# A hybrid decoder step on one core: softmax scaling shared by two query blocks, later loads of left down weights, and keys of both maps split in one operation

## The chip, the cores and the metric

The kernel runs on one core of one Trainium2 chip. The metric is the device time of one execution in microseconds (us): the median of three runs of the kernel before is 1473.42 us (1473.18 to 1474.27).

## The reference, cut to what matters

One layer of a decoder trunk is computed in fp32 for a prompt of 1024 rows and eight sample rows, with a model width of 1024. It consists of a mixer with four heads of differential attention and four heads of retention, a cross-attention into 256 memory rows, a squared-ReLU MLP of width 4096, and a last norm. Two parts of it concern the change. The first is the differential attention of the prompt, causal and with a relative bias, with two softmax maps per head of 64 columns of keys each:

```python
def probs(qi, ki):
    s = jnp.einsum('bqhd,bkhd->bhqk', qi, ki).astype(f32) * scale + bias
    return jax.nn.softmax(jnp.where(mask, s, neg), axis=-1)

attn = probs(q1, k1) - lam * probs(q2, k2)
return jnp.einsum('bhqk,bkhd->bqhd', attn, v.astype(f32))
...
a = head_rms(oa) * subln.astype(jnp.float32) * (1.0 - lam_init)
```

The second is the MLP, of which the product with `w_down` is the last stage:

```python
def sq_relu_mlp(h, w_up, w_down):
    return jnp.square(jax.nn.relu(h @ w_up)) @ w_down
```

## The kernel before

**Products.** Every fp32 product is made of three TensorE products of parts: each operand is split into a high part (a rounding copy, on ScalarE) and a low part (a subtraction of the high part from the whole, on VectorE), and high times high, high times low and low times high are added in PSUM (`mm3`, L75). Most of the rows that ScalarE (ACT) and VectorE (DVE) run are such splits.

**Attention.** The four heads run one after another between about 245 and 455 us. A list of 40 items (head, pair of query blocks, group of key blocks) is walked by the loop over `g` near L1380; `x` is the item's number within its head. At each item the loop issues scores of some query block and map (`scores`, L999, where `SCORES` says which), the transposes of the next item (`turn`, L1037; tile `trA`, with its high and low parts `ah` and `al`), and the weighing of values (`weigh`, L1058; tile `av`). Products of the next head's projection (`qkp`) fill the gaps on TensorE (PE). A scheduler then orders the instructions of each engine; what stands in an engine's queue runs in that order.

`scores(h, q, m)` computes the block of 128 queries `q` against the `128(q+1)` keys that the mask leaves, for map `m`: PE writes `sp` from the key stacks `KA[m]` and `KB[m]` and the query stack `Q[m]`, DVE adds the bias and takes the row's extreme (L1019), and ACT takes the exponential with its row sum (L1025). The map's tile is `e_h_q_m`. For `m` = 1, DVE then takes a reciprocal of the second map's sum (L1032), forms the scaling with `nlam` and the first map's sum (L1033), and adds the scaled second map onto the first, in place (L1034). That last row's length is `128(q+1)` columns. The tile of the second map has the tag `e1` with two buffers.

The stacks serve both parts of a key in one product: `KA[m]` holds the high part of map `m`'s 64 rows twice (rows 0 to 63 and 64 to 127), `KB[m]` the low part twice, and `Q[m]` the high part of the queries in one half and the low part in the other. `load_part` (L961) makes them, first for 688 columns and later for 336: for each map an ACT copy of 64 rows (L967), a transfer of it to the other half issued on GpSimd's queue (L968), a DVE subtraction (L969), a transfer (L970). GpSimd (POOL) also runs the memsets of `ah` and `al`, a power function for norms (L141) and the low parts of values (L995).

The norm over a head's output uses `norm_sums` (L1075): ACT squares the outputs of the head before (`sq_0` during head 1, and so on) into a tile that has the same tag `e1`, so that it takes the buffer of the second map of block 6 of the running head; then eight products with a column of ones write `ct` (L1084).

**Down product.** It runs from about 1134 us in four passes (`g` = 0 to 3), by a Strassen-like scheme with seven products `q` of half matrices. Left operands are weights, loaded as `raw_d` (L2492) and split into `wd` (L2388, L2389). Right operands are hidden values, loaded as `raw_h` in two pieces per product from `HT` or `HQ` in device memory (L2375) and split into `UH` and `UL` (L2381, L2382). PE writes `dn` into one of eight PSUM banks in turn (L2412), and DVE adds the bank onto the sums `c` (L2546), which frees it. All these loads are issued by SyncE's queue (SP), which runs in order. `load_left` issues a pass's eight `raw_d` loads.

## Time and profile before

| What | Value |
|---|---|
| Median of three runs | 1473.42 us |
| Profiled execution, its time / its span | 1475.19 us / 1473.4 us |
| PE busy | 1455.7 us, 99% of the span |
| DVE busy | 1107.9 us, 75% |
| ACT busy | 679.7 us, 46% |
| POOL busy | 314.4 us, 21% |
| Mean granted clock of PE | 0.996 |

The profile is one execution. Its time is 1.8 us more than its span, and 1.8 us more than the median of the runs. A row of a timeline has the start and the length in us, the engine, the line of the program, the operation, what it writes and reads (buffer numbers left out), and, in brackets, how long the engine was idle before it and what released it. PE rows of matmuls overlap in their ends. The stages follow from the lines: projections until about 245 us, attention to 455 us, the rest of the mixer and the memory part, the up product, and the down product from 1134 us.

### The profile page before, as it was taken

What the parts mean: (1) busy time and instruction counts of PE and PEld (TensorE: products, weight loads), DVE (VectorE), ACT (ScalarE), POOL (GpSimd) and SP (SyncE); (2) the same over time, 40 slices, a digit from 0 to 9 for tenths busy, and PEclk for the clock granted to TensorE, in tenths of its full rate; (3) what the DMA queues carried; (4) which work ended last, traced back from release to release, by engine and by line L of the source; (5) the groups of instructions that cost most, each with busy time, mean ns of one, the idle gap of its engine ahead of it and who ended that gap; (6) DMA issues with size and microseconds to landing.
All of it is one profiled execution on the core that took longest, in us unless ns stands there. A gap on an engine that the chain in (4) does not pass through costs nothing.

```text
span 1473.4 us, 28129 instructions
## 1 busy us (share of the span) xinstructions
PE 1455.7 (99%) x11013; PEld 1401.0 (95%) x11013; DVE 1107.9 (75%) x2263; ACT 679.7 (46%) x1327; POOL 314.4 (21%) x345
## 2 busy tenths in 40 slices
PE   9999999999999999999999999999999999999998
PEld 7899779999889999999999999999999999999998
DVE  7666536888867756567868988888888878787876
ACT  7434435666552441267436533343435443343454
POOL 0035433122304511224122000000002211110380
PEclk9999999999999999999999999999999999999998
DMA  8155738215957265654762444333446764536273
GB/s 295 62 188 171 205 70 192 72 34 159 283 169 269 100 209 170 177 178 122 236 234 77 151 159 158 138 136 133 149 159 216 262 213 144 173 105 200 71 130 116
DMA packets 129833, 238.98 MB, mean 162 GB/s; under 512 B 13606, under 2 KB 80987, under 8 KB 129572
## 3 DMA queue, kind: packets, MB, share of 16 engines
q1 hardware_dynamic: 91354, 170.66, 36.0%
q0 software_dynamic: 27472, 46.93, 11.8%
q10 hardware_dynamic: 10874, 19.60, 3.5%
q8 instruction: 86, 1.41, 0.4%
q14 instruction: 47, 0.39, 0.1%
HBM read 171.13 MB, written 58.92 MB: 156 GB/s over the span
## 4 chain that ended last, share of the span: by engine, by line
PE 88%; DVE 5%; DMA 2%; ACT 2%; issue 1%; POOL 0%; ACTq 0%; SPq 0%; DVEq 0%
PE dn L2412 20%; PE Z L2244 9%; PE qkp L75 6%; PE Y L2244 6%; PE X L2244 6%; PE mq L75 6%; PE pr_m L75 6%; PE pr_o L75 5%; PE grp L75 3%; PE sp L75 2%; PE mv L75 2%; PE mk L75 1%; PE av L75 1%; PE mpv L75 1%; PE vap_z L524 1%; PE vrp_z L524 1%
## 5 line engine op out<-in xcount | busy, mean ns | idle before, releaser
L2412 PE MATMUL dn<-UH,wd 128*128 128x258 f32 (+1 forms) x1800 | 326.6, 283 | 3.0 <-DVE c L2546 3.0
L2412 PEld LDWEIGHTS dn<-UH,wd 128*128 128x128 f32 x1800 | 279.6, 190 | 3.6 <-ACT wd L2388 2.6
L2412 PE MATMUL dn<-UL,wd 128*128 128x258 f32 x900 | 254.6, 283 | 0.0
L2412 PEld LDWEIGHTS dn<-UL,wd 128*128 128x128 f32 x900 | 170.5, 189 | 0.1
L2546 DVE TENSOR_TENSOR c<-c,dn 128x258 f32<-128x258 f32 (+1 forms) x217 | 89.1, 417 | 38.5 <-PE dn L2412 35.8
L2270 ACT ACTIVATE hq<-r 128x258 f32<-128x258 f32 x128 | 53.7, 421 | 117.4 <-DVE r L2269 117.3
L2244 PE MATMUL Z<-T_h,wu 128*128 128x258 f32 x512 | 98.1, 283 | 0.0
L2244 PE MATMUL X<-UH,wu 128*128 128x258 f32 x512 | 97.5, 282 | 0.0
L2388 ACT CAST wd<-raw_d 128x512 fp32r<-128x512 f32 x96 | 58.7, 619 | 82.0 <-PE dn L2412 77.3
L2052 ACT CAST wu<-raw_up 128x512 fp32r<-128x512 f32 x96 | 59.0, 616 | 61.0 <-PE Z L2244 52.6
L2381 ACT CAST UH<-raw_h 128x1032 fp32r<-128x1032 f32 x56 | 58.7, 1055 | 55.2 <-PE dn L2412 27.9
L2244 PEld LDWEIGHTS X<-UH,wu 128*128 128x128 f32 x512 | 81.3, 188 | 0.0
L2244 PEld LDWEIGHTS Z<-T_h,wu 128*128 128x128 f32 x512 | 81.3, 189 | 0.0
L2382 DVE TENSOR_TENSOR UL<-raw_h,UH 128x1032 fp32r<-128x1032 f32 x56 | 72.9, 1301 | 9.9 <-ACT UH L2381 9.9
L2389 DVE TENSOR_TENSOR wd<-raw_d,wd 128x512 fp32r<-128x512 f32 x96 | 72.3, 759 | 10.2 <-ACT wd L2388 10.2
L2281 POOL DMA_DIRECT2D HT<-ht x32 | 17.2, 536 | 292.1 <-DVE ht L2280 291.6
L2244 PE MATMUL Z<-T_l,wu 128*128 128x258 f32 x256 | 72.3, 282 | 0.0
L2244 PE MATMUL X<-UL,wu 128*128 128x258 f32 x256 | 72.3, 282 | 0.0
L129 ACT CAST wh_u<-raw_u 128x1024 fp32r<-128x1024 f32 x43 | 44.7, 1047 | 57.6 <-PE mq L75 39.9
L2053 DVE TENSOR_TENSOR wu<-raw_up,wu 128x512 fp32r<-128x512 f32 x96 | 64.8, 689 | 3.6 <-ACT wu L2052 3.6
L2402 POOL TENSOR_TENSOR raw_d<-raw_d,raw_d 128x512 f32<-128x512 f32 x16 | 22.1, 1384 | 197.0 <-DVE raw_d L2398 145.3
L130 DVE TENSOR_TENSOR wl_u<-raw_u,wh_u 128x1024 fp32r<-128x1024 f32 x39 | 48.6, 1257 | 20.2 <-ACT wh_u L129 20.0
(616 smaller groups left out, 4707.4 us busy)
## 6 DMA issues: line engine op xcount, KB each, us to landing
raw_u<-in_wall SPq DMA_DIRECT2D x49, 512.0 KB
HT<-ht POOLq DMA_DIRECT2D x32, 516.0 KB, 3.0
raw_h<-HT SPq DMA_DIRECT2D x32, 516.0 KB
raw_up<-in_wall SPq DMA_DIRECT2D x32, 512.0 KB
raw_d<-in_wall SPq DMA_DIRECT2D x32, 512.0 KB
HQ<-hq ACTq DMA_DIRECT2D x32, 387.0 KB
raw_h<-HQ SPq DMA_DIRECT2D x24, 516.0 KB
cmk<-in_cmk SPq DMA_DIRECT2D x16, 512.0 KB
```

What stands on the lines that cost most here:

```text
L75: pinned(nc.tensor.matmul(out, l, r, start=start, stop=stop))
L130: (lo_engine or nc.vector).tensor_sub(wl[:, :n], raw[:, :n], wh[:, :n].bitcast(F32))
L2052: nc.scalar.copy(w[:, :512], src)
L2053: nc.vector.tensor_sub(w[:, 512:], src, w[:, :512].bitcast(F32))
L2244: pinned(nc.tensor.matmul(ps, l, r[:, k, :], start=first and k == 0 and x == 0, stop=k == 3 and x == 2, skip_group_check=True))
L2270: nc.scalar.activation(h[:, PLACE[quad], :], r, AF.Square)
L2381: nc.scalar.copy(h, rv)
L2382: nc.vector.tensor_sub(l, rv, h.bitcast(F32))
L2388: nc.scalar.copy(w[:, :512], src)
L2389: nc.vector.tensor_sub(w[:, 512:], src, w[:, :512].bitcast(F32))
L2412: pinned(nc.tensor.matmul(ps[:, part], l, r[:, k, cq], start=first and k == 0 and x == 0, stop=k == 3 and x == 2, skip_group_check=True))
L2546: nc.vector.tensor_add(y, y, ps)
```

## The change

There are three edits.

**Keys.** For heads 1 to 3, one ACT copy of 128 rows writes both maps' high parts into `KA[1]`, and one DVE subtraction of 128 rows writes both low parts into `KB[1]`. Two transfers on GpSimd's queue bring map 0's half from there into both halves of `KA[0]`, two more into both halves of `KB[0]`, and with each query split one more transfer copies map 1's half within `KA[1]` or `KB[1]`. Head 0 is loaded as before. For each part there are six transfers where there were four, one ACT copy where there were two, and one DVE subtraction where there were two.

**Scaling.** The scaling and the addition onto the first map are left out for even query blocks and made with those of the odd block that follows: one reciprocal and one scaling of two columns serve both, then two additions run, the even block's first.

**Down weights.** In the pass `g` = 1, the eight `raw_d` loads are put behind the last load that was issued so far on SP's queue.

```diff
--- before.py
+++ after.py
@@ -961,7 +961,17 @@
         def load_part(h, cs):
             KA, KB, Q, _ = stacks[h]
             qraw, kraw = raws[h]
-            for m in range(2):
+            lo, hi = slice(0, 64), slice(64, 128)
+            if h:
+                nc.scalar.copy(KA[1][:, cs], kraw[:, cs])
+                for x in (lo, hi):
+                    nc.gpsimd.dma_start(KA[0][x, cs], KA[1][lo, cs])
+                nc.vector.tensor_sub(KB[1][:, cs], kraw[:, cs], KA[1][:, cs].bitcast(F32))
+                yield
+                for x in (lo, hi):
+                    nc.gpsimd.dma_start(KB[0][x, cs], KB[1][lo, cs])
+                yield
+            for m in range(0 if h else 2):
                 own = slice(64 * m, 64 * m + 64)
                 oth = slice(64 - 64 * m, 128 - 64 * m)
                 nc.scalar.copy(KA[m][own, cs], kraw[own, cs])
@@ -974,6 +984,9 @@
                 oth = slice(64 - 64 * m, 128 - 64 * m)
                 nc.scalar.copy(Q[m][own, cs], qraw[own, cs])
                 nc.vector.tensor_sub(Q[m][oth, cs], qraw[own, cs], Q[m][own, cs].bitcast(F32))
+                if h:
+                    K1 = (KA, KB)[m][1]
+                    nc.gpsimd.dma_start(K1[lo, cs], K1[hi, cs])
                 yield
 
         vraws = {}
@@ -1027,11 +1040,15 @@
             )
             seen["ACT"] = nc.cur_bb.bb.instructions[-1]
             if m:
-
-                e0 = es[h, q][0]
-                nc.vector.reciprocal(mn[:, 2:3], sm[:, 1, q : q + 1])
-                nc.vector.scalar_tensor_tensor(mn[:, 3:4], mn[:, 2:3], nlam, sm[:, 0, q : q + 1], ALU.mult, ALU.mult)
-                nc.vector.scalar_tensor_tensor(e0[:, :n], e[:, :n], mn[:, 3:4], e0[:, :n], ALU.mult, ALU.add)
+                es[h, q] += (e,)
+            if m and q % 2:
+                nc.vector.reciprocal(mn[:, 2:4], sm[:, 1, q - 1 : q + 1])
+                nc.vector.scalar_tensor_tensor(mn[:, 2:4], mn[:, 2:4], nlam, sm[:, 0, q - 1 : q + 1], ALU.mult, ALU.mult)
+                for x in range(2):
+                    e0, _, e1 = es[h, q - 1 + x]
+                    w = P * (q + x)
+                    nc.vector.scalar_tensor_tensor(
+                        e0[:, :w], e1[:, :w], mn[:, 2 + x : 3 + x], e0[:, :w], ALU.mult, ALU.add)
                 seen["E"] = nc.cur_bb.bb.instructions[-1]
 
         def turn(h, pr, kg):
@@ -2492,7 +2509,8 @@
                         nc.sync.dma_start(raws[p][x][:, :1024], i["wall"][U_DN + 8 * g + 2 * p + x])
                 seen["SP"] = nc.cur_bb.bb.instructions[-1]
 
-            load_left((0, 1) if g == 0 else range(4))
+            with tc.issue_after(seen["SP"]) if g == 1 else nullcontext():
+                load_left((0, 1) if g == 0 else range(4))
             S, W, bank, copied = {}, {}, {}, {}
 
             parts = [((1, 2), (1, 2), (0, 1)), ((), (1, 2), (2, 3)), ((6,), (6,), (0, 1)), ((), (6,), (2, 3))]
```

On ACT in head 2, around the square of head 1's outputs (`sq_1`; `e_2_7_1` is the exponential of block 7's second map, `raw_o0` a unit of weights for a later product), the order before is:

```order
L1025 ACTIVATE e_2_7_0_3999,sm_2_3471<-e_2_7_0_3999,mn_2_7_4000 128x1024
L1077 ACTIVATE sq_1_4038<-oraw_1_3286 128x1024
L1052 CAST ah_2_2_1_4063<-trA_2_2_1_4058 128x512
L967 CAST KA0_3_4048<-kraw_3_3695 64x688
L1025 ACTIVATE e_2_7_1_4022,sm_2_3471<-e_2_7_1_4022,mn_2_7_4000 128x1024
L967 CAST KA1_3_4049<-kraw_3_3695 64x688
L129 CAST wh_u40_4155<-raw_o0_4117 128x1024
L1052 CAST ah_2_2_2_4123<-trA_2_2_2_4119 128x384
```

and now it is:

```order
L1038 ACTIVATE e_2_7_0_3974,sm_2_3455<-e_2_7_0_3974,mn_2_7_3975 128x1024
L1038 ACTIVATE e_2_7_1_3997,sm_2_3455<-e_2_7_1_3997,mn_2_7_3975 128x1024
L966 CAST KA1_3_4025<-kraw_3_3674 128x688
L1069 CAST ah_2_2_1_4039<-trA_2_2_1_4034 128x512
L129 CAST wh_u40_4131<-raw_o0_4092 128x1024
L1094 ACTIVATE sq_1_4014<-oraw_1_3271 128x1024
L1069 CAST ah_2_2_2_4098<-trA_2_2_2_4094 128x384
```

The square stood ahead of the second map's exponential, with one copy for the keys behind it; it now stands behind the exponential, the copy for the keys, `ah_2_2_1` and the cast of `raw_o0`.

On DVE in head 1, around the scores of block 7's second map (`KB` are the low parts of head 2's keys, `c8` columns for the norm, `al_1_2_1` the low part of a transposed item; rows of `mn` alone read an accumulator), the order before is:

```order
L1034 SCALAR_TENSOR_TENSOR e_1_6_0_3369<-e_1_6_1_3394,mn_1_6_3370,e_1_6_0_3369 128x896
L1019 ISA e_1_7_1_3448,mn_1_7_3423<-sp_1_7_1_0_3449,M_1_2934 128x512
L1019 ISA mn_1_7_3423 128x1
L969 TENSOR_TENSOR KB0_2_3474<-kraw_2_3127,KA0_2_3472 64x688
L1019 ISA e_1_7_1_3448,mn_1_7_3423<-sp_1_7_1_1_3453,M_1_2934,mn_1_7_3423 128x512
L1019 ISA mn_1_7_3423 128x1
L1053 TENSOR_TENSOR al_1_2_1_3488<-trA_1_2_1_3482,ah_1_2_1_3487 128x512
L969 TENSOR_TENSOR KB1_2_3475<-kraw_2_3127,KA1_2_3473 64x688
L1032 RECIPROCAL mn_1_7_3423<-sm_1_2936 128x1
L1088 TENSOR_TENSOR c8_0_3516<-ct_0_3507,c8_0_3516 128x8
```

and now it is:

```order
L1032 ISA e_1_7_1_3431,mn_1_7_3406<-sp_1_7_1_0_3432,M_1_2926 128x512
L1032 ISA mn_1_7_3406 128x1
L1032 ISA e_1_7_1_3431,mn_1_7_3406<-sp_1_7_1_1_3436,M_1_2926,mn_1_7_3406 128x512
L1032 ISA mn_1_7_3406 128x1
L1103 RECIPROCAL c8_1_4067<-sm_1_2928 128x8
L1104 TENSOR_TENSOR c8_1_4067<-c8_1_4067 128x8
L969 TENSOR_TENSOR KB1_2_3459<-kraw_2_3114,KA1_2_3457 128x688
L1045 RECIPROCAL mn_1_7_3406<-sm_1_2928 128x2
L1046 SCALAR_TENSOR_TENSOR mn_1_7_3406<-mn_1_7_3406,nlam_88,sm_1_2928 128x2
L1050 SCALAR_TENSOR_TENSOR e_1_6_0_3355<-e_1_6_1_3380,mn_1_7_3406,e_1_6_0_3355 128x896
L1050 SCALAR_TENSOR_TENSOR e_1_7_0_3405<-e_1_7_1_3431,mn_1_7_3406,e_1_7_0_3405 128x1024
L1070 TENSOR_TENSOR al_1_2_1_3472<-trA_1_2_1_3466,ah_1_2_1_3471 128x512
```

The addition for block 6 (`e_1_6_0`) has moved from ahead of the second map's scores of block 7 to behind them, one row ahead of that of block 7, and the low part `al_1_2_1` stands behind both. In heads 0 and 2 the additions for blocks 6 and 7 stand together in the same way.

On SP in the down product, from the loads of pass 0's product 5 on (`raw_h0_3_0` and `raw_h0_3_2` are the two pieces of the right operand of its last product, 3; `raw_d1` are the weights of pass 1; `c12` are residual rows), the order before is:

```order
L2361 DMA c21_13487<-X3_73 128x4x516
L2375 DMA raw_h0_5_0_14176<-HT_75 128x4x258
L2375 DMA raw_h0_5_2_14180<-HT_75 128x4x258
L2492 DMA raw_d1_0_0_14436<-in_wall 128x1024
L2492 DMA raw_d1_1_0_14438<-in_wall 128x1024
L2375 DMA raw_h0_3_0_14184<-HQ_74 128x4x258
L2492 DMA raw_d1_2_0_14440<-in_wall 128x1024
L2375 DMA raw_h0_3_2_14188<-HQ_74 128x4x258
L2361 DMA c12_13489<-X3_73 128x516 x4
L2492 DMA raw_d1_0_1_14437<-in_wall 128x1024
L2492 DMA raw_d1_3_0_14442<-in_wall 128x1024
```

and now it is:

```order
L2378 DMA c21_13455<-X3_73 128x4x516
L2392 DMA raw_h0_5_0_14144<-HT_75 128x4x258
L2392 DMA raw_h0_5_2_14148<-HT_75 128x4x258
L2392 DMA raw_h0_3_0_14152<-HQ_74 128x4x258
L2392 DMA raw_h0_3_2_14156<-HQ_74 128x4x258
L2378 DMA c12_13457<-X3_73 128x516 x4
L2509 DMA raw_d1_0_0_14404<-in_wall 128x1024
L2509 DMA raw_d1_0_1_14405<-in_wall 128x1024
L2509 DMA raw_d1_1_0_14406<-in_wall 128x1024
L2509 DMA raw_d1_1_1_14407<-in_wall 128x1024
L2509 DMA raw_d1_2_0_14408<-in_wall 128x1024
L2509 DMA raw_d1_3_0_14410<-in_wall 128x1024
```

The loads of `raw_d1_0_0`, `raw_d1_1_0` and `raw_d1_2_0`, which stood ahead of the two pieces of product 3, and an earlier one, `raw_d1_1_1`, now stand behind them and behind the rows of `c12`.

## The prediction

> **What bounds the kernel now.** I read the page first, then what TensorE (PE) waits for, then the two places that the change touches.
>
> ```profile
> PE 1455.7 (99%) x11013; PEld 1401.0 (95%) x11013; DVE 1107.9 (75%) x2263; ACT 679.7 (46%) x1327; POOL 314.4 (21%) x345
> ```
>
> Of the span of 1473.4 us PE is busy for 1455.7, so no more than some 18 us of idle time and what the clock loses can be won, and the change adds or removes no PE work. What counts is each PE wait that comes or goes. The waits of PE by releaser begin so:
>
> ```profile
> PE dn L2412 <- DVE c L2546: 3.0, 2, 2.4
> PE trA L78 <- DVE e L1034: 2.1, 2, 1.4
> PE sp L75 <- DVE mn L1019: 1.8, 2, 1.0
> ```
>
> The columns after the colon are the total, the number and the longest. The largest single wait, 2.4 us, is in the down product, and two of these lines, 3.9 us together, are waits for the score rows and additions that the scaling edit touches. Any other DVE or ACT time that the change saves is off PE's path.
>
> **The down loads.** The next fences show PE's rows around the 2.4 us, the chain that leads to it, and the clock behind it.
>
> ```profile
> 1185.60 0.28 PE L2412 MATMUL dn<-UH,wd 128*128 128x258 f32 x1
> 1188.26 0.36 PE L2412 MATMUL dn<-UH,wd 128*128 128x258 f32 x1 [2.38 <-DVE c L2546]
> 1188.81 0.28 PE L2412 MATMUL dn<-UL,wd 128*128 128x258 f32 x1
> 1189.17 0.41 PE L2412 MATMUL dn<-UL,wd 128*128 128x258 f32 x1
> 1189.81 0.42 PE L2412 MATMUL dn<-UL,wd 128*128 128x258 f32 x1
> ```
>
> ```profile
> 1163.76 3.88 DMA raw_h<-HT
> ...
> 1170.01 5.21 DMA raw_h<-HT
> ...
> 1177.60 7.84 DMA raw_h<-HQ
> ...
> 1185.46 1.06 ACT UH L2381
> ...
> 1186.55 1.23 DVE UL L2382
> 1187.78 0.34 DVE c L2546
> ```
>
> ```profile
> 1189.00:1190.00 1.00, 1.00 (x7) 1.00 (x6) 1.00 (x4) 0.00 (x0) 0.00 (x0) 0.58 0.99 389
> ...
> 1192.00:1193.00 1.00, 1.00 (x8) 1.00 (x8) 0.00 (x0) 0.42 (x1) 0.00 (x0) 0.72 1.08 362
> ```
>
> PE stops because the bank that it wants is freed by an addition to `c` that stands on DVE behind the low part of the last piece of product 3, and that piece's transfer took 7.84 us. A like piece took 3.88 us at 1163.76. The long one, and the 5.21 us before it, ran beside the `raw_d` loads that now go behind. The third number from the right in a row of windows is the granted clock: 0.5 for (1 - 0.58)/0.5 = 0.84 us, for all of the two windows between, which stand at 0.50, and for (1 - 0.72)/0.5 = 0.56 us, 3.4 us in all. Between PE's rows of one form, three matmuls take 0.36 us (1188.81 to 1189.17) and then 0.64 (1189.17 to 1189.81). At 0.213 us each, 16 matmuls fit into 3.4 us, which would have taken 16 x 0.12 = 1.9 us: the slow stretch costs 1.5 us.
>
> In the new order the two pieces have the queue to themselves. With 3.88 us for the piece at 1170.01, it lands at 1173.9; its cast (1.06) and low part (1.23) end at 1176.2, which lets the last piece go (1177.60 in the trace). It lands at about 1180.1, and its low part ends at 1182.4. The order on DVE behind it is an addition, the low part of a weight and the addition that PE needs, two additions of 0.34 and a row that I estimate at 0.7, half of the low part of a whole piece and a little: 1.4 together, to 1183.8, while PE arrives at 1185.9. So 2 us of margin, and the wait and its slow clock both go: 2.4 + 1.5 = **-3.9 us**. If the last piece still began at 1177.60 and took 3.88, it would be 1.4 us later and still in time. If it took 5.21 from there, the wait would be some 0.6 us. If it took 7.84, the wait would be about 0.9 us longer than now (1185.44 + 2.3 + 1.4 = 1189.1 against 1188.26), because of the weight's low part ahead of the addition.
>
> ```profile
> 1201.54 0.62 ACT L2388 CAST wd<-raw_d 128x512 fp32r<-128x512 f32 x1 [1.24 <-PE dn L2412]
> ```
>
> The weights that are sent back belong to pass 1, and this cast of one, like those behind it, waits for PE's buffers and not for a load. I cost their delay at nothing. What hides it is that PE begins pass 1 only after these casts; without that cover each late load would cost up to a transfer, 3.9 us.
>
> [...]
>
> **The scaling, at the square.** `sq` takes the buffer of block 6's second map, whose reader, the addition for block 6, now stands behind the exponential of block 7. In head 1:
>
> ```profile
> 318.96 1.15 ACT L1025 ACTIVATE e<-e,mn 128x1024 f32<-128x1024 f32 x1
> 320.01 0.19 ACT L1025 ACTIVATION_READ_ACCUMULATOR e<-e,mn 128x1 f32 x1
> 320.10 1.05 ACT L1077 ACTIVATE sq<-oraw 128x1024 f32<-128x1024 f32 x1
> 321.64 0.77 ACT L967 CAST KA<-kraw 64x688 fp32r<-64x688 f32 x1
> ```
>
> ```profile
> 312.52 0.16 DVE L1032 RECIPROCAL mn<-sm 128x1 f32<-128x1 f32 x1
> ...
> 313.25 0.21 DVE L1033 SCALAR_TENSOR_TENSOR mn<-mn,nlam,sm 128x1 f32<-128x1 f32 x1
> ...
> 318.76 1.14 DVE L1034 SCALAR_TENSOR_TENSOR e<-e,mn,e 128x896 f32<-128x896 f32 x1
> ```
>
> ```profile
> 319.00 0.40 PE L75 MATMUL sp<-KB,Q 128*128 128x512 f32 x1
> 322.74 1.50 PE L75 MATMUL ct<-ones,sq 128*128 128x1 f32 x13
> ```
>
> Before, the square ended at 321.15, 1.6 us ahead of `ct`. Now ACT runs the first map's exponential (to 320.0), the keys' copy (0.7) and the second map's exponential, which ends with its sum at 321.9. PE's scores for it end at 319.4, and DVE, free of the block 6 addition and of one key subtraction, has reduced them by 320.2. Then come DVE's two small rows (0.37), the addition (1.1, to 323.35) and the square (1.0, to 324.4). PE is at `ct` at 322.74 and waits: **+1.6 us**, with 1.9 if each row's full length counts, and 0 if the square could end where it did.
>
> In head 2:
>
> ```profile
> 363.19 0.39 PE L75 MATMUL sp<-KB,Q 128*128 128x512 f32 x1
> 366.77 1.84 PE L75 MATMUL ct<-ones,sq 128*128 128x1 f32 x16
> ```
>
> ```profile
> 364.26 1.06 ACT L1077 ACTIVATE sq<-oraw 128x1024 f32<-128x1024 f32 x1
> ...
> 368.41 1.05 ACT L129 CAST wh_u<-raw_o 128x1024 fp32r<-128x1024 f32 x1
> ```
>
> PE's scores end at 363.6. With the 0.8 us that the reduction took in head 1's reckoning and an exponential of 1.15, the exponential ends at 365.6; behind it on ACT stand the keys' copy (0.77 in head 1), `ah` (estimated at 0.5, half of a cast of 1024 columns) and the cast of `raw_o0` (1.05), then the square (1.05), to 369.0. PE wants it at 366.77: **+2.2 us**, between 1.5 and 2.6.
>
> ```profile
> 395.97 0.55 PE L78 MATMUL trA<-ident,e 128*128 128x128 f32 x3 [1.40 <-DVE e L1034]
> ```
>
> ```profile
> 395.00:399.00 4.00, 3.03 (x31) 2.58 (x32) 4.00 (x13) 1.51 (x3) 0.36 (x1) 1.00 1.09 402
> ```
>
> Whether the half clock follows is bounded by two rows, the 2.38 us that it followed and the 1.40 us above, behind which the window from 395 to 399 us has a clock of 1.00. I take the nearer row for each: none behind 1.6, and 1.5 us behind 2.2, so **+1.5 us**. [...]
>
> In head 0 there is no square, and in head 3 its products come much later than it; I take 0 for both.
>
> **The rest of attention.** These rows of PE and DVE bear on it:
>
> ```profile
> 262.42 0.41 PE L75 MATMUL sp<-KA,Q 128*128 128x320 f32 x1 [0.85 <-DVE mn L1019]
> 331.55 0.27 PE L78 MATMUL hrT<-ident,c 128*8 128x128 f32 x1 [0.25 <-DVE c L1086]
> 359.34 0.38 PE L78 MATMUL trA<-ident,e 128*128 128x128 f32 x2
> 414.71 0.42 PE L75 MATMUL pr_half<-UH,wh_u 128*128 128x344 f32 x1 [0.61 <-DVE x_half L1356]
> ```
>
> ```profile
> 357.99 1.02 DVE L1034 SCALAR_TENSOR_TENSOR e<-e,mn,e 128x768 f32<-128x768 f32 x1
> ```
>
> Three waits become shorter: 0.85 us for scores loses the 0.37 of two small rows, 0.25 us for `hrT` is covered by the later PE, and 0.61 us for `pr_half` waits for a DVE row that no longer has block 6's addition ahead. Together -1.2. Against that, the addition of block 4 now stands right ahead of that of block 5, which PE's transposes want early in the next item: in head 2 the latter ended at 359.0 and PE came at 359.34, 0.3 us later. Block 4's addition is 5/6 as wide (0.85 us), and its small rows (0.37) are gone, so about 0.2 us is missing: +0.6 over three heads, and `al` behind both additions in head 0 gives +0.1. The sum is **-0.5 us**, between -2 and +1.5 (the longest waits for additions and scores, 1.4 and 1.0, could go either way: DVE is busy for all 4 us of the window above).
>
> **The keys.** The first row is the early transfers of low parts in head 1, with the median us to landing at its end, the row after it the first product of head 2 on map 1's keys.
>
> ```profile
> KB<-KB POOLq DMA_DIRECT2D x2, 172.0 KB, 5.1
> ```
>
> ```profile
> 335.42 0.28 PE L75 MATMUL sp<-KA,Q 128*128 128x256 f32 x1
> ```
>
> One DVE row and one ACT copy less per part are hidden anyway, since PE waits for neither. The twelve added transfers are issued on GpSimd's in-order queue, and the copies within `KA[1]` and `KB[1]` wait there for earlier ones to land; behind them stand the memsets of `ah` and `al` and the power function. In head 1 the last copy would go at about 329 and, landing in 5.1 us, be there by 334.5; the products that read it began at 335.42 and are 1.6 us later now. I take 0, with 2 us as the price of a landing that is late.
>
> **Sum.** -3.9 + 1.6 + 2.2 + 1.5 - 0.5 = +0.9 us on the profiled 1475.19, which lies 1.8 above the median; against the median, 1473.42 + 0.9 = 1474.3 us. A measurement of this kernel tells 0.2% (2.9 us) from no change, so this counts as the same.
>
> **Rivals.** *The square is in time after all* (faster): if the exponentials ran 1.5 us earlier, since DVE is less loaded, both waits fall below 0.7 us together and no half clock follows. For it: the square had 1.6 and 1.4 us of room. Against it: ACT's order alone puts two more rows ahead. It gives -3.9 + 0.7 - 0.5 = -3.7, 1469.7 us. *Both waits slow the clock* (slower): at 1.9 and 2.6 us, each with 1.5 behind it, and the rest at +0.2: -3.9 + 4.5 + 3.0 + 0.2 = +3.8, 1477.2 us; it decides from where a gap between 1.40 and 1.9 us is enough. The short `ct` rows of one column that follow each wait speak for it, the 1.40 us row against. *The last piece of product 3 still lands late* (slower, and the third edit does not do what its place suggests): nothing is won, the wait grows by 0.9, and 1473.42 + 0.9 + 3.9 + 0.9 gives 1479.1 us. For it: the transfer is as long as 7.84 us also because rows of `c` share the queue. Against it: the 3.88 us row, which had such rows behind it as well.
>
> **Chances.** The forecast has 0.46; its own range, with the bounds of the rest, is 1470.5 to 1476.3. The first rival has 0.24, the second 0.17 and the third 0.13. So faster 0.24, same 0.46, slower 0.30. The range reaches from just below the first rival to near the third, 1469.5 to 1478.5.
>
> **What would show it.** PE waits at `ct` of about 1.6 and 2.2 us in heads 1 and 2, released by ACT `sq`, with windows of half clock behind the second alone; no wait of over 0.5 us in pass 0 of the down product and no half clock there; `raw_h` transfers from `HQ` of about 4 us. The prediction is wrong where these waits at `ct` are missing, or where the wait for `c` near 1188 us is still there.

## The result, and the profile after

The changed kernel takes 1487.29 us, the median of 4 runs (1486.32 to 1487.46), against 1473.30 (1472.53 to 1474.27) for the kernel before: a ratio of 1.0093, 95% interval 1.0076 to 1.0111. It is slower by 0.9%, outside the range on record. The profiled execution took 1487.41 us, with a span of 1485.7 and a mean granted clock of 0.992 (0.996 before).

The first line is the page's line of busy times after, the others are the longest of TensorE's (PE) waits by releaser: total, number, longest.

```profile
PE 1463.0 (98%) x11013; PEld 1406.7 (95%) x11013; DVE 1099.0 (74%) x2225; ACT 675.6 (45%) x1321; POOL 314.4 (21%) x357
```

```profile
PE ct L75 <- ACT sq L1094: 4.1, 2, 2.3
PE av L75 <- DVE al L1070: 2.6, 2, 2.1
PE trA L78 <- DVE e L1050: 2.1, 2, 1.3
PE dn L2429 <- DVE c L2564: 1.5, 3, 0.6
PE sp L75 <- DVE mn L1032: 1.3, 2, 0.9
```

DVE and ACT have less to do, as meant, and nothing was won by it. The 2.4 us wait of the down product is gone, and `ct` heads the list. PE is busy for 7.3 us more with the same 11013 products, at a mean granted clock of 0.992 in place of 0.996.

These are PE's two waits for the square, and ACT's and DVE's rows that lead to the first:

```profile
325.17 1.00 PE L75 MATMUL ct<-ones,sq 128*128 128x1 f32 x6 [1.85 <-ACT sq L1094]
376.39 1.87 PE L75 MATMUL ct<-ones,sq 128*128 128x1 f32 x10 [2.26 <-ACT sq L1094]
```

```profile
322.81 2.35 DVE L1050 SCALAR_TENSOR_TENSOR e<-e,mn,e 128x896 f32<-128x896 f32 x2
```

```profile
322.14 0.19 ACT L1038 ACTIVATION_READ_ACCUMULATOR e<-e,mn 128x1 f32 x1
322.23 0.57 ACT L1069 CAST ah<-trA 128x512 fp32r<-128x512 f32 x1
324.06 1.06 ACT L1094 ACTIVATE sq<-oraw 128x1024 f32<-128x1024 f32 x1 [1.26 <-DVE e L1050]
```

The exponential's sum ends at 322.3, the first of the two additions lets the square go at 324.06, and it ends at 325.1: the chain of the prediction, 0.7 us later than it was put there (324.4), with PE 0.4 us later too.

What follows the waits was not as predicted. The next view shows windows of time: length, PE's busy time, the other engines', and, third from the right, the granted clock. It is divided into stretches of 3.413 us.

```profile
322.27:325.68 3.41, 1.56 (x13) 1.27 (x11) 3.25 (x5) 1.58 (x3) 1.13 (x3) 1.00 1.03 255
325.68:329.09 3.41, 3.41 (x16) 3.41 (x17) 0.42 (x3) 0.00 (x0) 1.16 (x4) 0.50 0.59 118
329.09:332.51 3.42, 3.42 (x15) 3.36 (x15) 1.86 (x4) 1.86 (x3) 1.89 (x2) 0.50 0.40 79
...
373.47:376.88 3.41, 1.15 (x10) 0.87 (x8) 3.34 (x6) 2.86 (x4) 1.49 (x4) 1.00 0.73 219
376.88:380.29 3.41, 3.41 (x16) 3.41 (x17) 1.35 (x4) 0.00 (x0) 1.54 (x3) 0.50 0.60 149
380.29:383.71 3.42, 3.42 (x14) 3.42 (x13) 0.67 (x2) 0.00 (x0) 1.67 (x1) 0.50 0.05 17
...
400.78:404.19 3.41, 2.43 (x26) 1.40 (x24) 3.35 (x10) 1.57 (x4) 1.60 (x4) 1.00 1.17 331
404.19:407.61 3.42, 3.42 (x16) 3.42 (x15) 2.73 (x12) 2.41 (x8) 1.12 (x3) 0.50 1.16 366
```

Behind each `ct` wait stand two stretches of half clock, and a third place, behind a wait for scores in head 3, has one. The half clock begins and ends on the boundaries of these stretches, which I call the grid: from 325.68 to 376.88 are 15 stretches of 3.413 us, and from there to 404.19 are 8. It holds to the end of the profile: the next half clock begins at 1479.39, which is 338 stretches behind 325.68.

How much later PE stands after, against a second profile of the kernel before whose execution (1472.99 us) is near its median (experiment 5), from the same product in both:

| Up to | PE later by, us | What came in between |
|---|---|---|
| 323.0 | 0.4 | small waits of heads 0 and 1 |
| 325.2 | 2.5 | `ct` wait, head 1 |
| 332.6 | 5.7 | its half clock |
| 373.8 | 7.2 | additions of head 2's second pair late (0.78 and 1.31 us against one wait of 0.7) |
| 376.4 | 9.7 | `ct` wait, head 2 |
| 383.9 | 12.9 | its half clock |
| 408.0 | 14.7 | scores in head 3 (0.93 us) with half clock |
| 446.9 | 13.9 | a wait for an addition gone (-1.6), one of 2.13 for `al` new (+1.4), -0.6 |
| end | 14.4 | the down pass: +0.5 |

The theory from this: each part has its own price, the late square's with two windows of half clock is 10.9 us, the rest of attention 3.0, and the down pass won nothing against a usual execution. Rivals: the keys edit carries a good part; the longer additions cost wherever they stand; or the square is only a sign of a late ACT.

### The profile page after: what moved, and what is told of

Its sections match the earlier page's. It is cut to its first block, busy times and chain, and to the rows that moved or that the text cites. A ratio compares the mean times of both kernels' runs of the same rounds, so it can differ in the third digit from the quotient of the medians.

```text
span 1485.7 us, 28127 instructions
## 1 busy us (share of the span) xinstructions
PE 1463.0 (98%) x11013; PEld 1406.7 (95%) x11013; DVE 1099.0 (74%) x2225; ACT 675.6 (45%) x1321; POOL 314.4 (21%) x357
## 3 DMA queue, kind: packets, MB, share of 16 engines
q8 instruction: 86, 1.41, 0.4%
## 4 chain that ended last, share of the span: by engine, by line
PE 86%; DVE 7%; DMA 2%; ACT 2%; issue 2%; POOL 0%; SPq 0%; DVEq 0%; ACTq 0%
PE dn L2429 19%; PE Z L2261 9%; PE mq L75 6%; PE pr_m L75 6%; PE qkp L75 6%; PE X L2261 6%; PE Y L2261 6%; PE pr_o L75 5%; PE grp L75 3%; PE av L75 1%; PE sp L75 1%; PE mpv L75 1%; PE vap_z L524 1%; PE vrp_z L524 1%; PE mk L75 1%
## 5 line engine op out<-in xcount | busy, mean ns | idle before, releaser
L75 PE MATMUL qkp<-UH,wh_u 128*128 128x344 f32 x192 | 64.3, 335 | 0.1
```

The source lines that it names most:

```text
L75: pinned(nc.tensor.matmul(out, l, r, start=start, stop=stop))
```

## The experiments

The comparisons are each with runs of the kernel before on the same chip, whose median lay between 1473.07 and 1474.12 us.

**1. The later down loads alone.**

```diff
-            load_left((0, 1) if g == 0 else range(4))
+            with tc.issue_after(seen["SP"]) if g == 1 else nullcontext():
+                load_left((0, 1) if g == 0 else range(4))
```

> The kernel before with the later left down weights alone. Theory (each part of the change keeps its own price): the wait of the down product near 1188 us and the 3.4 us of half clock behind it go, 3.9 us, and up to 0.9 us comes back as new short waits of the down product for DVE's left unpacking, whose rows then stand beside POOL's: 1469.4 to 1470.4 us against 1473.3. Rival (the load's place is worth nothing by itself, since another operation becomes the late one): 1473.3 us, with a wait of over 1 us left at the same product.

Measured: 1473.28 us (10 runs), ratio 1.0003, 0.9993 to 1.0012. The wait near 1188 us is not there, as the theory had it, but the gain is not either. Experiment 5 says why.

**2. The keys edit alone** (the first two hunks of the diff).

> The kernel before with the keys of both maps split in one operation alone; the order of the squares on ACT is as before. Theory: the edit is worth nothing by itself, 1473.3 us within 1.5, and TensorE's waits for ct and the two pairs of half-clock windows at heads 1 and 2 are not there. Rival (the split and its transfers carry the loss): 1478 us or more.

Measured: 1476.54 us (7 runs, 1472.66 to 1480.61), ratio 1.0027, 1.0014 to 1.0040. Between the two: no wait for `ct` and no half clock behind one, but 3 us slower in most runs. The profile is of the run of 1472.66 us (experiment 6 has another).

**3. The shared scaling alone** (the third hunk).

> The kernel before with the shared scaling of two query blocks alone; the squares of heads 1 and 2 stand behind the second map's exponentials on ACT. Theory (this edit carries the whole loss): TensorE waits about 2 us for ct in head 1 and in head 2, each followed by two windows of half clock (6.8 us, of which 3.2 us is lost); with the later additions' other waits 1485 to 1491 us, 12 to 18 above the kernel before. Rival (only the two waits come with it, and the half clock is from the keys edit's other timing): under 1479 us.

Measured: 1491.21 us, ratio 1.0127, 1.0110 to 1.0144. The two `ct` rows in it:

```profile
325.66 2.15 PE L75 MATMUL ct<-ones,sq 128*128 128x1 f32 x16 [2.82 <-ACT sq L1081]
375.26 3.57 PE L75 MATMUL ct<-ones,sq 128*128 128x1 f32 x16 [2.22 <-ACT sq L1081]
```

This edit carries the loss, and more of it than all three edits together: measured alone, the three add to some 21 us (17.8 for this one, 3.2 for the keys, 0 for the loads), and the changed kernel lost 14. Part of the difference is a wait that the changed kernel lacks: here PE waits 2.82 us for an addition at 408.47, with a half clock behind it, after DVE has waited 2.99 us for the transfer of the decoder's selection. In the changed kernel that row waits 0.59 us. Behind the first wait there is one window of half clock (327.26 to 330.67), behind the second there are two.

**4. The changed kernel with blocks 6 and 7 each scaled by itself.**

```diff
-            if m and q % 2:
+            first = q - 1 if q % 2 and q < 6 else q
+            if m and (q % 2 or q == 6):
...
-                for x in range(2):
+                for x in range(q - first + 1):
```

> The changed kernel, but query blocks 6 and 7 are scaled each by itself as before; blocks 0 to 5 still share. The square of block 6's sums then stands ahead of the second map's exponentials again. Theory (the late square makes the waits for ct and these start the half-clock windows): both ct waits and the four windows behind them go, about 10 us, to 1475 to 1479 us; what is left against the kernel before is the other waits in attention less the 3.9 us of the down pass. Rival (sharing costs as such, by the longer additions on DVE wherever they stand): 1484 us or more.

Measured: 1480.37 us, ratio 1.0055, 1.0038 to 1.0071, so 7 us less than the changed kernel. Both `ct` waits and their half clock are gone. The time lies a little above what was expected, since other waits stand in its place:

```profile
349.81 0.30 PE L78 MATMUL trA<-ident,e 128*128 128x128 f32 x1 [0.79 <-DVE e L1052]
351.42 0.55 PE L78 MATMUL trA<-ident,e 128*128 128x128 f32 x3 [1.31 <-DVE e L1052]
390.59 0.84 PE L78 MATMUL trA<-ident,e 128*128 128x128 f32 x3 [1.04 <-DVE e L1052]
400.63 0.30 PE L78 MATMUL trA<-ident,e 128*128 128x128 f32 x1 [3.08 <-DVE e L1052]
```

The next two fences are DVE's and POOL's rows ahead of these waits:

```profile
347.99 3.38 DVE L1052 SCALAR_TENSOR_TENSOR e<-e,mn,e 128x384 f32<-128x384 f32 x2
...
388.79 0.69 DVE L1156 TENSOR_TENSOR oraw<-oraw,rbh 128x512 f32<-128x512 f32 x1 [1.73 <-DMA rbh<-hrow]
389.40 0.21 DVE L1048 SCALAR_TENSOR_TENSOR mn<-mn,nlam,sm 128x2 f32<-128x2 f32 x1
...
399.14 0.21 DVE L1247 TENSOR_SCALAR dmn<-dmn,qblkd 128x1 f32<-128x1 f32 x1 [3.25 <-DMA qblkd<-in_sel]
399.27 0.21 DVE L1048 SCALAR_TENSOR_TENSOR mn<-mn,nlam,sm 128x2 f32<-128x2 f32 x1
...
399.87 1.28 DVE L1052 SCALAR_TENSOR_TENSOR e<-e,mn,e 128x384 f32<-128x384 f32 x2
```

```profile
347.96 1.28 POOL L1008 TENSOR_TENSOR VL<-vraw,VH 128x512 fp32r<-128x512 f32 x1 [3.37 <-ACT VH L1006]
349.55 1.26 POOL L1008 TENSOR_TENSOR VL<-vraw,VH 128x512 fp32r<-128x512 f32 x1 [0.31 <-ACT VH L1006]
```

Two things are to be seen. The two additions of 384 and 512 columns take 1.28 us at 399.87 and 3.38 at 347.99, where POOL's subtractions begin 0.03 us ahead of them and run for 2.54. And the shared scaling row stands, in DVE's order, behind rows that wait for a transfer: the row factors (1.73 us) and the decoder's selection (3.25 us). In the first profile of before, the scaling and the addition of head 3's block 0 ran at 383.25 and 383.51, ahead of the row for the factors at 385.80.

**5. The kernel before once more**, unchanged, for a second profile.

> The kernel before once more, unchanged, for a second profile. Theory (the half clock is decided by a free-running window of 3.41 us, so what stands behind one and the same wait differs from run to run): the down product near 1188 us waits about 2.4 us again, but with half clock behind it in about one run of three only, and head 3's wait for the row minimum at 390 us may have the half clock instead. Rival (the run is the same each time): both as in the first profile, wait 2.4 us and 3.4 us of half clock behind it. If the wait itself is much shorter than 2 us, the later left down weights had less to win than one profile showed.

Measured: 1472.99 us. The wait near 1188 us is missing. Its waits of the down product, all of them:

```profile
PE dn L2412 <- ACT c L2543: 0.7, 1, 0.7
PE dn L2412 <- DVE c L2546: 0.6, 1, 0.6
```

The low parts of product 3's two pieces on DVE, first in the first profile, then in this one:

```profile
1183.87 1.23 DVE L2382 TENSOR_TENSOR UL<-raw_h,UH 128x1032 fp32r<-128x1032 f32 x1 [4.69 <-ACT UH L2381]
1186.55 1.23 DVE L2382 TENSOR_TENSOR UL<-raw_h,UH 128x1032 fp32r<-128x1032 f32 x1 [0.18 <-ACT UH L2381]
```

```profile
1182.02 1.24 DVE L2382 TENSOR_TENSOR UL<-raw_h,UH 128x1032 fp32r<-128x1032 f32 x1 [2.04 <-ACT UH L2381]
1184.97 1.24 DVE L2382 TENSOR_TENSOR UL<-raw_h,UH 128x1032 fp32r<-128x1032 f32 x1 [0.45 <-ACT UH L2381]
```

With the same program the pieces were 1.6 to 1.9 us earlier and PE came to the product 1.4 us later (1187.27 against 1185.88), so it did not wait there at all. Of nine profiles here with the loads in their old place (the two of before and experiments 2, 3, 6 and 11 to 14), only the first has a wait of over 1 us in the down product. The 3.9 us were there to be won in that execution, not in the usual one.

**6. The keys edit alone once more.**

> The kernel with the keys edit alone once more, for a second profile, since its times lay between 1472.7 and 1480.6 us and the first profile was of the fastest run. Theory (the edit's new transfers on POOL's queue make later transfers land at uneven times): a run near 1477 us shows one new wait for a transfer of 1 us or more that the first profile lacks, with half clock behind it. Rival (only the position of the half-clock windows differs): the same waits as in the first profile, and more windows of half clock.

Measured: 1476.40 us, one run. PE waits 2.26 us at 427.04 for the buffer of `trA`, with one window of half clock, where experiment 2's profile has no wait. ACT's row there in this run, then in experiment 2:

```profile
422.52 1.99 ACT L129 CAST wh_u<-raw_o 128x1024 fp32r<-128x1024 f32 x2 [2.94 <-DMA raw_o<-in_wall]
```

```profile
420.03 2.00 ACT L129 CAST wh_u<-raw_o 128x1024 fp32r<-128x1024 f32 x2 [0.78 <-DMA raw_o<-in_wall]
```

As the theory had it, a load that ACT waits for in its order lands later in one run than in another. That it is the keys' transfers that delay it, this run does not show.

**7. The products for `ct` one place later in heads 1 and 2**, the square as late as in the changed kernel.

```diff
-NORM_AT = (2, 3, 4, 5, 8), (2, 5, 6, 8, 9)
+NORM_AT = (2, 4, 5, 6, 8), (2, 5, 6, 8, 9)
```

> The changed kernel, but with the products for ct, the row factors made from them and the row one place later in TensorE's order in heads 1 and 2. The squares stay as late as in the changed kernel. Theory (TensorE's wait for the late square and the half clock behind it are the loss): both waits under 0.5 us, no half clock near 326 and 377 us, about 10 us less, 1476 to 1479 us. Rival (the late square is only a sign of ACT's later work, which holds something else as long): 1484 us or more.

Measured: 1484.61 us, ratio 1.0076, 1.0060 to 1.0093. Both `ct` waits are gone and no half clock stands at 326 or 377 us, but only 2.7 us were won, and the time is as the rival gave it. The time came back at another place, since the row factors follow `ct` and now arrive later, in the middle of DVE's work for head 3:

```profile
397.63 1.29 DVE L1154 TENSOR_TENSOR oraw<-oraw,rbh 128x512 f32<-128x512 f32 x2 [2.72 <-DMA rbh<-hrow]
```

```profile
399.45 0.63 PE L75 MATMUL sp<-KA,Q 128*128 128x320 f32 x1 [3.46 <-DVE mn L1032]
```

PE waits 3.46 us there, and three windows of half clock stand in this profile (from 354.8, 399.2 and 440.1).

**8. The products for `ct` with 64 columns instead of one.**

```diff
-                mm(ct[:, x : x + 1], sq[:, x * P : x * P + P], ones[:, :1], True, True)
+                mm(ct[:, 64 * x : 64 * x + 64], sq[:, x * P : x * P + P], ones.to_broadcast([P, 64]), True, True)
...
-            nc.vector.tensor_mul(c8[:, 2, :], ct[:, :8], c8[:, 1, :])
+            nc.vector.tensor_mul(c8[:, 2, :], ct[:, ::64], c8[:, 1, :])
```

> The changed kernel, but each product for ct streams 64 equal columns instead of one; only the first of each 64 is used. The waits stay. Theory (a window of 3.41 us is followed by half clock if its products stream under about a third of the columns it has time for, and one-column products stream next to nothing): behind each ct wait the second window of half clock goes, 1.5 us each, 1483.5 to 1485.5 us. Rival (a window counts as busy by the number of its products, or the wait alone sets the length): 1486.5 to 1488 us with 6.8 us of half clock behind each ct wait.

Measured: 1484.73 us, ratio 1.0080, 1.0064 to 1.0097. The number came as expected, the places did not:

```profile
323.80:327.21 3.41, 2.01 (x17) 2.01 (x18) 2.00 (x3) 1.06 (x1) 0.00 (x0) 1.00 1.07 266
327.21:330.62 3.41, 3.41 (x14) 3.35 (x14) 1.49 (x5) 1.30 (x3) 3.00 (x5) 0.50 0.27 57
...
371.59:375.00 3.41, 1.17 (x9) 0.88 (x8) 3.19 (x5) 3.16 (x6) 1.48 (x4) 1.00 0.71 208
375.00:378.41 3.41, 3.41 (x17) 3.41 (x17) 2.11 (x4) 0.00 (x0) 1.54 (x3) 0.50 0.58 139
```

In head 1 the second window is gone, but there the `ct` rows ended before the window at 327.21 began. The half clock in head 3 is missing in this profile too. In head 2, where they fill the first slow window, the second one stayed (378.41 to 381.82, clock 0.50), although the rows are wider. So rows of 64 columns did not end the half clock here, and the gain is one of position. Whether wider rows would is open.

**9. Blocks 6 and 7 apart, and the waiting DVE rows behind** (experiment 4 and two groups of rows moved).

```diff
-NORM_AT = (2, 3, 4, 5, 8), (2, 5, 6, 8, 9)
+NORM_AT = (2, 3, 4, 5, 9), (2, 5, 6, 8, 9)
...
-            nc.vector.tensor_scalar(mn[:, 2:3], nlam, 1.0, None, ALU.subtract)
-            nc.vector.tensor_scalar(mn[:, 2:3], mn[:, 2:3], second, 1.0, ALU.mult, ALU.add)
+            with tc.issue_after(seen["DVE"]):
+                nc.vector.tensor_scalar(mn[:, 2:3], nlam, 1.0, None, ALU.subtract)
+                nc.vector.tensor_scalar(mn[:, 2:3], mn[:, 2:3], second, 1.0, ALU.mult, ALU.add)
```

> The kernel with query blocks 6 and 7 apart (1480.4 us), and two groups of DVE rows moved: the multiplications of a finished head by its row factors stand one place later in heads 1 and 2, and the two decoder rows that read the loaded selection stand behind the decoder's scores. Theory (what is left of the loss without the ct waits is that the shared additions now stand in DVE's order behind rows that wait for a transfer, 1.6 us at 388 and 3.1 us at 400 us with 1.5 us of half clock behind it): those waits go, 1473.5 to 1476 us. Rival (the longer additions themselves are late wherever they stand): 1479 us or more.

Measured: 1476.83 us (10 runs, 1473.23 to 1478.86), ratio 1.0023, 1.0013 to 1.0032: 3.5 us less than experiment 4, 0.8 above the range given. At the end of attention (431.5 us) PE stands where it does in experiment 5, within 0.01 us. So the whole loss of attention is accounted for in this profile. Its 3.6 us come later, at memory products (0.8 each at 519 and 648, 1.1 at 654) and in the down pass.

**10. The same, with the low parts of all values (`VL`, both column halves) formed on DVE.**

```diff
-                eng = nc.vector if h == 3 and cs.start == 0 else nc.gpsimd
-                eng.tensor_sub(VL[:, cs], vraw[:, cs], VH[:, cs].bitcast(F32))
+                nc.vector.tensor_sub(VL[:, cs], vraw[:, cs], VH[:, cs].bitcast(F32))
```

> The kernel of the run before, and the left halves of the values of every head formed on DVE instead of POOL. Theory (POOL's subtraction holds up the additions beside it, 3.4 us for two rows that take 1.3 us alone): the 1.4 us of waits for the additions at head 2's second pair go too, about 1 us less than that run, 1472.5 to 1475 us. Rival (the 0.7 us rows on DVE cost what they save): equal to it or slower.

Measured: 1477.34 us, ratio 1.0029, 1.0019 to 1.0038: no gain over experiment 9. The wait that it was to remove was already gone there, as the moved rows had changed the moment of the additions. In experiment 9 both additions began ahead of POOL's first subtraction: they took 1.27 us, and that subtraction, begun 0.2 us after the second of them, 1.69 in place of 1.28. The run tells nothing on what POOL's part costs PE.

**11. The kernel before with the low parts of all values on DVE** (the same edit).

> The kernel before with the left halves of the values of every head formed on DVE instead of POOL, nothing else. Theory: TensorE's waits for an addition beside POOL's subtraction (0.7 and 1.4 us at 349 and 396 us) shrink by 1 us or more together, 1471 to 1472.5 us against 1473.3. Rival (DVE's queue is the late one and takes the rows' 0.7 us each): 1473 us or more.

Measured: 1472.82 us, ratio 0.9997, 0.9988 to 1.0007. Against experiment 5 the two waits shrank from 0.74 and 1.41 us to 0.16 and 0.42, and a new one of 0.51 stands at 359.57; at the end of attention PE is 0.7 us ahead, too little to tell in runs that scatter over 4 us. No version here is measurably faster than the kernel before.

**12. The kernel before with a transfer of the keys issued twice** in heads 1 to 3, six transfers for each part instead of four.

```diff
                 nc.gpsimd.dma_start(KA[m][oth, cs], KA[m][own, cs])
+                if h:
+                    nc.gpsimd.dma_start(KA[m][oth, cs], KA[m][own, cs])
```

> The kernel before with the transfer of the right keys' halves issued twice in heads 1 to 3, so that six transfers stand for each part of a head's keys as in the keys edit, not four; the splits stay apart. Theory (the keys edit alone was 3 us slower in most runs because its two more transfers of 64 rows each delay the loads that ACT waits for near 420 us): 1475 us or more. Rival (the transfers are hidden and the keys edit's loss is in its order of rows): 1473.3 us within 1.

Measured: 1476.29 us, ratio 1.0020, 1.0010 to 1.0029. Two more transfers for each part alone cost what the keys edit costs, though they are not the same transfers: they write a half a second time. The place is not the one expected: in this profile DVE waits for an output's transfer out of the keys' tile, and PE for the addition behind it.

```profile
384.78 0.21 DVE L1197 TENSOR_SCALAR qblkd<-relb 32x128 f32<-32x128 f32 x1 [3.19 <-DMA out_kT<-kraw]
```

```profile
390.41 0.44 PE L78 MATMUL trA<-ident,e 128*128 128x128 f32 x2 [1.68 <-DVE e L1036]
```

In experiment 5 that DVE row began at 381.55. Of the 3.7 us by which this profile ends later than that of experiment 5, 1.5 come at a half clock from 770.99 to 774.40, in the stretch before which PE waits nowhere for more than 0.3 us.

**13. Six blocks shared, the waiting rows behind, without the keys edit and the later loads.** The edit is that of experiments 4 and 9 on the kernel before.

> The kernel before with three things only: blocks 0 to 5 share their scaling, and the two groups of DVE rows of the run with rows behind are moved. The keys edit and the later loads are left out. Theory (with the square early and the waiting rows behind the additions the shared scaling costs nothing; the 3.5 us that were left are the keys edit's two more transfers per part): 1472 to 1474 us. Rival (the 3.5 us belong to the shared scaling or the moved rows): 1475.5 us or more.

Measured: 1474.58 us (12 runs), ratio 1.0003, 0.9995 to 1.0012. It lies 0.6 above the range given, but the kernel before took 1474.12 us beside it, and the ratio is the theory's. The shared scaling of the first six blocks costs nothing once no waiting row stands ahead of it, and it wins nothing either. What experiment 9 lost beyond this goes with the keys edit, as the later loads cost nothing in experiment 1; that is a difference of two runs, and parts did not simply add elsewhere (experiment 3).

**14. All eight blocks shared, `ct` later, the waiting rows behind**, without the keys edit and the later loads (experiment 3, with `NORM_AT` of (2, 4, 5, 6, 9) in its first list, and the decoder's rows as in experiment 9).

> The kernel before with all eight blocks sharing in pairs, the products for ct and what follows one place later in heads 1 and 2, and the two groups of DVE rows moved; no keys edit, no later loads. Theory (the late square costs only where TensorE meets the products for ct early, and the rest is the waiting rows): 1473 to 1477 us against 1491.2 for the shared scaling alone. Rival (the last pair's additions, 1.8 us of DVE in one piece behind the last exponential, are late by themselves): 1480 us or more, with waits for the additions or the products of values at each head's end.

Measured: 1480.30 us, ratio 1.0045, 1.0030 to 1.0060: 10.9 us less than experiment 3, and at the rival's bound. Neither theory has the remaining 6 us right. No wait for an addition is left, but with `ct` later the row factors are late again:

```profile
392.85 1.29 DVE L1141 TENSOR_TENSOR oraw<-oraw,rbh 128x512 f32<-128x512 f32 x2 [1.70 <-DMA rbh<-hrow]
```

```profile
395.75 0.41 PE L75 MATMUL sp<-KA,Q 128*128 128x320 f32 x1 [2.60 <-DVE mn L1019]
433.26 0.39 PE L75 MATMUL av<-al,VH 128*128 128x256 f32 x1 [2.13 <-DVE al L1057]
```

The second wait, of 2.13 us, is in the changed kernel and in experiments 3 and 7 too, and in none where blocks 6 and 7 are apart; experiment 8 shares all blocks and lacks it. DVE's order tells them apart: in these four runs the row that ends head 2's norm (`c`, L1117 in the changed kernel) and waits 1.6 us for POOL's power function stands ahead of `al`, and in the other twelve profiles behind it. No run moves that row alone. Another 1.5 us of this profile come at a half clock from 772.94, as in experiment 12.

## Why the prediction was wrong

**The down loads, -3.9.** In the profile that it was read from, it held to the tenth: from the product before that wait to the ones behind it PE gains 3.9 us, and no half clock is left there. Against a usual execution it was worth nothing (experiments 1 and 5). The failed step is not the reckoning of transfers but the sum that set a median against them. The text said that the profiled execution lay 1.8 us above the median, and still took the wait's price off the median as if every run had it. The margin of 2 us that it reckoned for the moved loads was not what decided: the wait was absent with the loads in their old place.

**The square, +1.6 and +2.2.** Right in mechanism and size: 1.85 and 2.26 us, released by `sq`.

**The half clock, "none behind 1.6, and 1.5 us behind 2.2".** This is the step that failed most: it cost 3.2 us behind each wait, 6.4 in place of 1.5. The two bounding rows were compared by the length of the wait. In these traces the length alone does not decide; the half clock goes with what PE starts in one stretch of the grid (the last section counts it). In the changed kernel the longest of these waits but one, 2.13 us, has no half clock:

```profile
442.97 0.39 PE L75 MATMUL av<-al,VH 128*128 128x256 f32 x1 [2.13 <-DVE al L1070]
```

```profile
438.32:441.74 3.42, 2.52 (x18) 2.30 (x16) 1.93 (x3) 2.21 (x3) 1.46 (x1) 1.00 0.18 54
441.74:445.15 3.41, 2.18 (x15) 2.17 (x16) 2.19 (x4) 0.00 (x0) 0.34 (x2) 1.00 0.16 54
```

It began at 440.84, and the grid's boundary at 441.74 divides it. The 1.85 us wait lay within one stretch, and so did the 2.26. Behind each of them a second stretch stayed slow, where the 2.38 us wait of before had one: in head 1 as in head 2, 11 of the 16 one-column `ct` rows, which the prediction named as a reason for its second rival, stand in the first slow stretch. Experiments 3 and 8 agree (the latter with rows of 64 columns): with most of these rows in the first slow stretch a second one follows (head 2 of both), with at most two of them there it does not (head 1). That rival, both waits with a half clock, had the right sign, a chance of 0.17 and 3.0 us; with two windows to each wait it is 6.4.

The stretches ahead of the half clock were not idle: PE was busy in them for 1.56 and 1.15 us.

**The rest of attention, -0.5.** It was +3.0, and the table has its parts: the additions of head 2's second pair (+1.5), the scores in head 3 with their half clock (+1.8), the new 2.13 us wait for `al` (+1.4) and small waits early on (+0.4), against a wait for an addition that went (-1.6) and 0.6 behind it. The part that failed is the price of a deferred row: the prediction set it at 0.2 us in each of three heads, for blocks 4 and 5, and priced neither the other pairs nor what stands on DVE ahead of the rows that PE wants.

The pair in head 2 ran beside POOL's subtractions and took 3.37 us, for two rows that take 1.3 otherwise. In experiment 4 it took 3.38 us beside 2.54 us of POOL's subtractions, where the pair in head 3, with POOL idle, took 1.28. What this alone costs PE was not separated (experiments 10 and 11). The 2.13 us wait goes with a row that stands ahead of `al` and waits for POOL (experiment 14).

Waits of deferred additions behind rows that wait for a transfer, 1.7 and 3.3 us in experiment 4, are shown to cost time by moving those rows alone (experiment 9 against 4: -3.5 us, and attention level with before). But they are the loss of experiment 4 and, with 2.99 us, part of that of experiment 3. In the changed kernel, where PE is 13 us later by then, the same rows wait 0.6 us at most for a transfer.

**The keys, 0.** Alone the edit costs 0.27% (0.14 to 0.40), and experiment 12, where two added transfers for each part cost as much, makes these the likely cause. The price named for a late landing, 2 us, was of the right size, but at the wrong place: not the stack's own products wait, but rows on DVE and ACT that wait for other transfers. Which of them is late differs from run to run, and how a delay at 390 us or after becomes the 3 us at the end is open. In the changed kernel the edit's share cannot be told from the rest, since the three edits together cost 7 us less than the sum of each alone.

**In sum.** Against the usual execution: +10.9 for the square with its half clock (forecast 5.3), +3.0 in the rest of attention (-0.5), +0.5 in the down pass (-3.9), 14.4 us. The waits for the square and their half clock are shown to be the cause of their part by experiments 4 and 7, in which they go, and by 3, in which they come with the scaling alone. The time they take does not simply come back when they go: 7 us did in experiment 4 and 2.7 in experiment 7, as other rows then came late.

## What to carry to other kernels

Before a wait of one profile is counted as a gain, see that it is there in a second one, above all where it hangs on a transfer and the profiled execution lies above the median. When a row is put off, read the whole engine order between its old place and its new one, for rows that wait for a transfer and for buffers whose next writer then comes late. Do not price a wait of the busiest engine by its length alone: here one of 2.13 us cost no more than itself, with a clock of 1.00 behind it, and one of 1.85 us cost 5, with two stretches at 0.50.

## What the runs showed of the hardware

The half clock does not follow the length of a wait. In the changed kernel it follows a wait of 0.93 us in head 3, where 16 of the 26 products in that stretch are the decoder's, 0.63 us in all; in the profiles of before the same wait, 0.98 and 0.61 us long, has none, and in experiment 1, with 0.97, it has. With one program the clock fell in one run and not in another: behind the same 0.97 us wait experiment 2's profile has a half clock at 391.11, and experiment 6's has none. The grid lies otherwise in the two. In experiment 2 the boundary stands just behind the wait (390.08 to 391.05); in experiment 6 the half clock behind the 2.26 us wait begins at about 427.85 by the spacing of PE's rows, so that I estimate a boundary 11 stretches ahead of it, at about 390.3, within the wait (390.12 to 391.09). That can be part of the scatter of 1470.9 to 1478.1 us of the kernel before; how much, no run shows.

Nor is it PE's busy time as the profile counts it. In experiment 8 the stretch with 2.01 us busy, nearly all in rows of 64 columns, was followed by half clock; in the changed kernel one with 1.78 us, of wide rows, was not:

```profile
352.99:356.40 3.41, 1.78 (x11) 1.34 (x9) 3.41 (x4) 1.93 (x5) 2.54 (x2) 1.00 0.05 16
```

Nor does it take a wait. In experiments 3, 10, 12 and 14 a stretch that begins between 767 and 782 us, with PE busy for 3.15 of its 3.41 us and no wait over 0.3, was followed by half clock; 16 of its products (`opm`) have 8 columns each.

What it goes with in these profiles is the number of columns. I add up the columns of the products that start in a stretch; the decoder's products in head 3 (`dsc`, of 128 columns), which start four at a time within 0.02 us, count a quarter each. The median of the full-clock stretches is 7224. In the sixteen profiles, without the first 8 and the last 15 us, 16 full-clock stretches have up to 1806 columns, and half clock follows each of them. Of the 12 with 1984 to 2708, it follows 8. Of the 6743 with more, it follows none. A third of the median, 2408, lies in the range where it follows some. In before, the stretch ahead of the half clock at 1189.15 has 1806. In the changed kernel the stretches with the two `ct` waits have 1725 and 1037, the slow ones behind them 1043 each, the one in head 3 2650, and the two that share the 2.13 us wait 4552 and 4504; in before, the stretch with the 1.40 us wait of the prediction has 2832. Sixteen products of 64 columns add 1024: in experiment 8 the stretch with all sixteen in head 1 has 1368, and the first slow one in head 2 has 1240, and half clock follows both. This is a count over the sixteen profiles; no run varies the columns alone, so it shows what goes together and no cause.
